# Attention sums by accumulating DMAs and column tiles of ones, in place of a third pass over the values

## The chip, the core and the metric

The kernel runs on one core of a Trainium2 chip. The metric is the device time of one execution in microseconds (us). Engines are named as the profile names them: PE (TensorE, matmuls), PEld (its weight loads), DVE (VectorE), ACT (ScalarE), POOL (GpSimd), SP (SyncE, which issues most DMAs).

## What is computed

One layer of a hybrid backbone over 128 prompt tokens and 1024 latent tokens, all in F32, width 1024. One projection gives queries, keys, values and gates of two mixers with 8 query heads of 64 and 2 key heads each (so a key head g serves 4 query heads). Mixer A is global attention, mixer B a band of 128 with a sink. The part that the change touches is mixer A:

```
def global_attn_latent(q, k_lat, v_lat, k_ctx, v_ctx):
    k_all = concatenate([k_ctx, k_lat]); v_all = concatenate([v_ctx, v_lat])    # 128 + 1024 keys
    s = einsum('bqkgd,bskd->bkgqs', qblk, k_all) * d ** -0.5                     # per block of 128 queries
    p = softmax(s, axis=-1)
    return einsum('bkgqs,bskd->bqkgd', p, v_all)
...
merge_out: concatenate([o_a * silu(g_a), o_b * silu(g_b)]) @ w_out
```

Prompt tokens attend to themselves alone, with the same weights.

## The kernel before

Matmuls take operands of type F32R. To keep F32's precision each operand is split in a high part and a low part (what is left of the value), and a product is made of several passes: high x high, high x low, low x high.

The kernel has a stage of modulation and projections (until about 303 us in the profile), the attention stage, and a short tail. Attention runs over 36 units (t, m, g): tile t of 128 tokens, mixer m (0 is A, 1 is B), key head g. For each latent tile and head an A unit is followed by a B unit; the two prompt pairs come last. A unit has 4 heads x 128 queries = 512 columns. An A unit of a latent tile has nine blocks of 128 keys, one *slot* each; a B unit has three or four. So an A unit with the B unit behind it makes a cycle of 13 slots, 12 at the first and the last latent tile.

In a slot of an A unit `scores` has TensorE make the transposed scores (keys on partitions, 512 columns) in two passes; ScalarE takes the exponential into a tile `pe` and casts it to the high part `ph`; the low part `pl` = pe - ph is made on GpSimd (L1131), for block 4 on VectorE (L1129). Three slots later (LAG) `values` runs the passes that multiply by the values and sum over all blocks in one PSUM bank `pv`. The stationary tile of A is `v_hi`: 64 columns of the values' high part, and 64 columns of ones beside them. The passes are

```
nc.tensor.matmul(pv, two, ph, start=(b == 0), stop=False)              # L1141: [values high | ones] by ph
if m == 0:
    nc.tensor.matmul(pv[0:64, :], vl, ph, start=False, stop=False)     # L1143: values low by ph, A alone
nc.tensor.matmul(pv, two, pl, start=False, stop=last)                  # L1144: [values high | ones] by pl
```

The ones give the row sums of the softmax in partitions 64 to 127 of `pv`, each of them 64 times. At a unit's end (END_AT, slots after the last block) ScalarE makes the inverse of the sums with a logarithm and an exponential (L1155, L1156), VectorE multiplies the values by it (L1165), GpSimd multiplies by the loaded gate `sgl` (L1167), ScalarE casts to `ogh` and GpSimd makes the low part `ogl` (L1179), and the output projection's passes (L1212) are laid into later slots, 2.5 a slot. For mixer B, `v_hi` has the values' high and low part side by side, two passes are enough, and the two halves of `pv` are added at the end; B's exponentials are made beside A's first four slots (`weight_items`) and its sums are handled apart. Passes that find a bound for the scores (`pmx`, L881) are laid into fixed slots.

Work is written down slot by slot: `tick()` first runs what `later(n, f)` put down for this slot, then come `scores`, what is due, output passes, and `values`. Every engine runs its instructions in the order of writing (`in_order`); an instruction that waits holds up all behind it on its engine. Buffers: PES = 3 tiles `pe`, 4 of `ph` and `pl` each, NOG = 5 pairs of gated outputs; PSUM banks A (2, small items), B (2, scores), C (2, `pv`), D and E.

Of the kernel before, what the change touches and what calls it, by code (L numbers as in the profile page):

```python
# [18 lines left out]
P = 128  # L19
# [16 lines left out]
PL_DVE = (4,)  # L36
LAG = 3
# [26 lines left out]
NOG = 5  # L64
PES = 3
# [43 lines left out]
def hybrid_step(ctx, tc, x_prompt, x_sample, cache_k_a, cache_v_a, cache_k_b, cache_v_b,  # L109
# [598 lines left out]
    v_lo = kv.tile([P, 20, HD], F32R, name="v_lo")  # L708
# [7 lines left out]
    def split_values(src, j):  # L716

        nc.vector.tensor_tensor(v_lo[:, j : j + 2, :], src[:, 0], v_hi[:, 0, j : j + 2, 0, :], op=ALU.subtract)
        nc.vector.tensor_tensor(v_hi[:, 1, j : j + 2, 1, :], src[:, 1], v_hi[:, 1, j : j + 2, 0, :], op=ALU.subtract)

    with tc.tile_pool(name="kt", bufs=2) as kt:
        W_GB.pools[WRAW : WRAW + 2] = [(kt, 2)] * 2
        sg_tile.append(lambda n: kt.tile([P, 512], F32, tag="kh", name=n, bufs=KEYS))
        for b in range(0, 20, 4):
            later(4 + b // 2, lambda b=b: nc.gpsimd.tensor_scalar(
                v_hi[:, 0, b : b + 4, 1, :], gain4, 0.0, 1.0, op0=ALU.mult, op1=ALU.add))
# [353 lines left out]
    w2 = ctx.enter_context(tc.tile_pool(name="w2", bufs=2, side="right"))  # L1080
    def blocks(t, m, g):

        if t == 0:
            k = (khp[:, g, :], klp[0:68, g, :]) if m == 0 else 0
            return [(k, v_hi[:, m, 18 + g], v_lo[:, 18 + g, :])]
        if m == 0:
            return [((kha[:, g, b, :], kla[:, g, b, :]), v_hi[:, 0, 2 * b + g], v_lo[:, 2 * b + g, :]) for b in range(9)]
        p0, p1_ = window(t)
        at = {p: b + 1 for b, p in enumerate(POS)}
        return [(p - p0, v_hi[:, 1, 2 * at.get(p, 0) + g], None) for p in range(p0, p1_)]  # L1090
# [16 lines left out]
    def scores(i, b, blk):  # L1107

        t, m, g = units[i]
        s = bank("B", f"st{i}_{b}")  # L1110
        ph, pl = parts_tiles(i, b)
        if m == 1:
            o = P * blk[0]
            for h in range(4):
                nc.tensor.transpose(s[:, P * h : P * h + P], penat[i][:, h, o : o + P], ident_r.bitcast(F32))  # L1115
            nc.scalar.copy(ph, s)  # L1116
            later(1, lambda: nc.vector.tensor_tensor(pl, s, ph, op=ALU.subtract))  # L1117
            return ph, pl
        kh, kl = blk[0]
        nc.tensor.matmul(s, kh, qtile[i], start=True, stop=False)  # L1120
        nc.tensor.matmul(s, kl, qbtile[i], start=False, stop=True)  # L1121
        pe = w3.tile([P, 512], F32, tag="pe", name=f"pe{i}_{b}", bufs=PES)
        nc.scalar.activation(pe, s, AF.Exp)  # L1123
        if i == 0 and b < PH_DVE:
            nc.vector.tensor_copy(ph, pe)
        else:
            nc.scalar.copy(ph, pe)  # L1127
        if b in PL_DVE:
            later(1, lambda: nc.vector.tensor_tensor(pl, pe, ph, op=ALU.subtract))  # L1129
        else:  # L1130
            nc.gpsimd.tensor_tensor(pl, pe, ph, op=ALU.subtract)  # L1131
        return ph, pl

    def values(i, b, last, blk, ph, pl):
        t, m, g = units[i]
        _, vh, vl = blk
# [5 lines left out]
        if m == 0:  # L1142
            nc.tensor.matmul(pv[0:64, :], vl, ph, start=False, stop=False)  # L1143
# [6 lines left out]
        def inverse():  # L1150
            v["rs"] = w2.tile([64, 512], F32, tag="rs", name=f"rs{i}", bufs=1)
            if m == 1:
                nc.scalar.copy(v["rs"], pv[64:128, :])
                return
            nc.scalar.activation(v["rs"], pv[64:128, :], AF.Ln)  # L1155
            nc.scalar.activation(v["rs"], v["rs"], AF.Exp, scale=-1.0)  # L1156

        def gated():
# [5 lines left out]
            for s in range(2):  # L1164
                nc.vector.tensor_tensor(of[64 * s : 64 * s + 64], pvv[:, :, s, :], srv[:, :, s, :],  # L1165
                                        op=ALU.add if m else ALU.mult)
            nc.gpsimd.tensor_tensor(of, of, sgl.pop(i), op=ALU.mult)  # L1167
            later(GATE_LATE, lambda: load_gate(i + 2))
            v["of"] = of
# [176 lines left out]
```

## Time and profile before

| | us |
|---|---|
| median of 2 runs (711.51 to 711.84) | 711.67 |
| the profiled execution | 711.52 |
| its span, first to last instruction | 709.6 |
| attention stage, first scores to the last latent tiles | 303 to 694 |

| engine | busy us of the span |
|---|---|
| PE | 691.6 |
| PEld | 558.5 |
| DVE | 469.3 |
| ACT | 409.9 |
| POOL | 334.2 |

Busy times are unions of the instructions' spans. TensorE's matmuls overlap, so that the duration of one (395 ns for 512 columns) is more than what it adds to a row of them; the distance between two starts tells that. DMAs count for no engine; their issue stands in the rows of the issuing queue (SPq, ACTq), with the time to landing. The granted clock of TensorE was 0.999 over the span. A row of a timeline is: start, duration, engine, line, operation, out<-in, count, and in brackets the idle time just before with the instruction that ended it.

### The profile page before, as it was taken

The numbers are of one execution on the slowest core, as the hardware profiler recorded it, in microseconds if no ns is written. First come the engines' busy times: TensorE is split into PE (matmuls) and PEld (weight loads), VectorE is DVE, ScalarE is ACT, GpSimd is POOL, SyncE is SP. The second block draws the span as 40 slices with busy tenths as digits, with TensorE's granted clock in tenths as the row PEclk, the third lists the DMA queues.
The fourth block names the chain that finished last, engine by engine and source line by source line (L and its number), as shares of the span: only waits on it lengthen the run. The fifth ranks groups of instructions, "written<-read, shape, count | busy, mean of one in ns | idle before, by whom it ended". The sixth has DMA issues, their size and how long they took to land. (4 is left out here: it accounts for less than half of the span.)

```text
span 709.6 us, 10604 instructions
## 1 busy us (share of the span) xinstructions
PE 691.6 (97%) x3508; PEld 558.5 (79%) x3508; DVE 469.3 (66%) x1019; ACT 409.9 (58%) x829; POOL 334.2 (47%) x356
## 2 busy tenths in 40 slices
PE   7999999999999999989999999999999999999987
PEld 4778988878787889966788888888888888787865
DVE  4667257967848945647867578666775776675662
ACT  5646412412403431188777887787778777877760
POOL 3547023233213421256756655665576557555660
PEclk9999999999999999999999999999999999999999
DMA  8962283358353116332222121212221221222323
GB/s 316 415 211 102 78 302 74 90 154 263 84 139 104 37 39 215 123 108 57 78 68 85 50 82 53 71 57 75 68 82 38 79 71 50 78 72 70 104 67 121
DMA packets 53560, 78.58 MB, mean 111 GB/s; under 512 B 7096, under 2 KB 25720, under 8 KB 52608
## 3 DMA queue, kind: packets, MB, share of 16 engines
q1 hardware_dynamic: 45328, 65.96, 28.1%
q10 hardware_dynamic: 8176, 11.94, 6.3%
q8 instruction: 28, 0.46, 0.3%
q14 instruction: 28, 0.23, 0.1%
HBM read 58.69 MB, written 19.18 MB: 110 GB/s over the span
## 5 line engine op out<-in xcount | busy, mean ns | idle before, releaser
L1131 POOL TENSOR_TENSOR pl<-pe,ph 128x512 fp32r<-128x512 f32 x130 | 167.7, 1292 | 145.0 <-DVE nm L942 67.5
L882 DVE TENSOR_REDUCE mx<-pmx 128x1 f32<-128x384 f32 x192 | 101.4, 552 | 56.3 <-PE pmx L881 54.8
L1123 ACT ACTIVATE pe<-st 128x512 f32<-128x512 f32 x146 | 86.8, 594 | 28.2 <-PE st L1121 27.4
L1127 ACT CAST ph<-pe 128x512 fp32r<-128x512 f32 x146 | 90.6, 621 | 4.8
L1141 PE MATMUL pv<-ph,v_hi 128*128 128x512 f32 x208 | 82.8, 398 | 2.2 <-DVE spare L1165 2.2
L1144 PE MATMUL pv<-pl,v_hi 128*128 128x512 f32 x208 | 82.4, 396 | 0.0
L1212 PE MATMUL po<-wo,ogh 128*128 128x512 f32 x216 | 72.6, 395 | 0.2 <-DVE yt L1219 0.2
L174 POOL TENSOR_TENSOR rs_q<-ms_q,mhalf 128x8 f32<-128x8 f32 x18 | 34.1, 1896 | 80.9 <-DVE ms_q L172 80.9
L942 DVE CUSTOM_DVE_ANT_0 sn<-sn,mask,nsink 128x512 f32<-128x512 f32 (+1 forms) x64 | 46.4, 724 | 38.0 <-PE sn L939 37.6
L881 PE MATMUL pmx<-kha,qt 128*128 128x384 f32 x192 | 61.2, 363 | 0.4 <-ACT pen L928 0.2
L1120 PE MATMUL st<-qt,kha 128*128 128x512 f32 x144 | 58.2, 404 | 1.9 <-ACT pe L1123 1.1
L1121 PE MATMUL st<-qb,kla 68*128 68x512 f32 x144 | 57.5, 399 | 1.1 <-DVE qb L901 1.1
L1143 PE MATMUL pv<-ph,v_lo 128*64 128x512 f32 x146 | 57.6, 395 | 0.0
L1144 PEld LDWEIGHTS pv<-pl,v_hi 128*128 128x128 f32 x208 | 39.2, 189 | 16.4
L928 ACT ACTIVATE pen<-sn,nm 128x512 f32<-128x512 f32 (+2 forms) x72 | 45.0, 626 | 6.5 <-DVE nm L942 3.1
L1116 ACT CAST ph<-st 128x512 fp32r<-128x512 f32 x62 | 36.4, 587 | 19.9 <-PE st L1115 18.7
L1141 PEld LDWEIGHTS pv<-ph,v_hi 128*128 128x128 f32 x208 | 39.3, 189 | 10.6 <-ACT ogh L1177 2.4
L646 ACT CAST qo0q<-ptq 128x512 fp32r<-128x512 f32 x18 | 10.6, 586 | 60.7 <-PE ptq L643 55.8
L1212 PEld LDWEIGHTS po<-wo,ogh 128*128 128x128 f32 x216 | 40.0, 188 | 6.8 <-DVE yt L1219 0.6
L1117 DVE TENSOR_TENSOR pl<-st,ph 128x512 fp32r<-128x512 f32 x62 | 42.5, 686 | 2.7 <-ACT ph L1116 2.1
L1212 PE MATMUL po<-wo,ogl 128*128 128x512 f32 x108 | 42.6, 394 | 0.0
L881 PEld LDWEIGHTS pmx<-kha,qt 128*128 128x128 f32 x192 | 35.6, 191 | 6.4 <-DVE mx L882 1.3
(213 smaller groups left out, 1699.2 us busy)
## 6 DMA issues: line engine op xcount, KB each, us to landing
qt<-qd SPq DMA_DIRECT2D x36, 256.0 KB, 3.0
wm<-in_w_mod_ss_dram SPq DMA_DIRECT2D x7, 1024.0 KB, 10.0
qd<-qo0q ACTq DMA_DIRECT2D x36, 128.0 KB, 2.4
qd<-qo1q ACTq DMA_DIRECT2D x36, 128.0 KB, 2.4
sgl<-gd SPq DMA_DIRECT2D x36, 128.0 KB, 2.2
out_dram<-yt SPq DMA_DIRECT2D x17, 256.0 KB, 2.0
xn<-in_x_sample_dram SPq DMA_DIRECT2D x8, 512.0 KB, 7.2
wg<-in_w_mod_g_dram SPq DMA_DIRECT2D x4, 1024.0 KB, 8.3
```

Source lines behind the costliest of these rows:

```text
L881: nc.tensor.matmul(pm[:, 0:384], lhs, kha[:, g, 3 * b : 3 * b + 3, :], start=True, stop=True)
L882: nc.vector.tensor_reduce(mx[:, h, b : b + 1], pm[:, 0:384], axis=AX.X, op=ALU.max)
L942: nc.vector.tensor_tensor_reduce(s, s, mask[:, m0 : m0 + n], -1.0, nsink[:, 4 * g + h : 4 * g + h + 1], op0=ALU.add, op1=ALU.min, accum_ou ...
L1120: nc.tensor.matmul(s, kh, qtile[i], start=True, stop=False)
L1121: nc.tensor.matmul(s, kl, qbtile[i], start=False, stop=True)
L1123: nc.scalar.activation(pe, s, AF.Exp)
L1127: nc.scalar.copy(ph, pe)
L1131: nc.gpsimd.tensor_tensor(pl, pe, ph, op=ALU.subtract)
L1141: nc.tensor.matmul(pv, two, ph, start=(b == 0), stop=False)
L1143: nc.tensor.matmul(pv[0:64, :], vl, ph, start=False, stop=False)
L1144: nc.tensor.matmul(pv, two, pl, start=False, stop=last)
L1212: nc.tensor.matmul(po[n], a, wo_parts[KT * n + k][lo], start=(k == KS[0] and p == 0), stop=(k == KS[-1] and p == 2))
```

## The change

In `v_hi` mixer A's values now stand as B's did: high part and low part side by side, with no ones. An A unit makes two passes a block, and the two halves of `pv` are added at the end for both mixers (ScalarE copies one, VectorE adds the other).

The row sums are made in another way. Two F32 tiles `acc` of 128x512 take turns. The exponentials of blocks 0 and 1 are written right into them; the tiles `pe` of blocks 2 to 8 are added to them by accumulating DMAs, SBUF to SBUF, issued from GpSimd a slot later. So `acc` holds, for each of 128 key positions, the sum over blocks. Then `row_sums` sums over partitions: the stationary tile is 128x32 of ones in F32, and four matmuls with 32 columns each fill the four quarters of a PSUM tile 128x256 (for a quarter, two of the four heads); one group for each of the two accumulators, 4 and 5 slots later (SUMS_AT). ScalarE makes the inverse with a logarithm and an exponential on 128x256, and GpSimd multiplies the gate `sgl` by it (a new product) before it multiplies the output by `sgl`. For the prompt units the one tile `pe` is summed without a DMA.

PES goes from 3 to 4, NOG from 5 to 4. The fill of ones in `v_hi` (five GpSimd instructions) becomes one memset, and the two subtractions that split the values become one.

```diff
+ADD_AFTER = 1
+PROMPT_SUMS = 2
+SUMS_AT = (4, 5)
-NOG = 5
-PES = 3
+NOG = 4
+PES = 4
...
-    v_lo = kv.tile([P, 20, HD], F32R, name="v_lo")
+    ones_v = kv.tile([P, 32], F32, name="ones_v")
...
-        nc.vector.tensor_tensor(v_lo[:, j : j + 2, :], src[:, 0], v_hi[:, 0, j : j + 2, 0, :], op=ALU.subtract)
-        nc.vector.tensor_tensor(v_hi[:, 1, j : j + 2, 1, :], src[:, 1], v_hi[:, 1, j : j + 2, 0, :], op=ALU.subtract)
+        nc.vector.tensor_tensor(v_hi[:, :, j : j + 2, 1, :], src, v_hi[:, :, j : j + 2, 0, :], op=ALU.subtract)
...
+    acc = [w2.tile([P, 512], F32, name=f"acc{n}", bufs=1) for n in range(2)]
...
-        pe = w3.tile([P, 512], F32, tag="pe", name=f"pe{i}_{b}", bufs=PES)
+        mine = acc[(i // 2 + b) % 2]
+        if t and b < 2:
+            pe = mine
+        else:
+            pe = w3.tile([P, 512], F32, tag="pe", name=f"pe{i}_{b}", bufs=PES)
         nc.scalar.activation(pe, s, AF.Exp)
...
+        if t == 0:
+            later(PROMPT_SUMS, lambda: row_sums(i, pe))
+        else:
+            later(ADD_AFTER, lambda: add_up(i, b, pe, mine))
         return ph, pl
+
+    summed, scaling = {}, {}
+
+    def add_up(i, b, pe, mine):
+        if b > 1:
+            nc.gpsimd.dma_start(mine, pe, accum_op=ALU.add)
+        if b > 6:
+            later(SUMS_AT[b - 7] - ADD_AFTER + (b == 7), lambda: row_sums(i, mine, b - 7, b == 8))
+
+    def row_sums(i, src, n=0, last=True):
+        if n == 0:
+            summed[i] = bank("A", f"ss{i}")[:, 0 : 2 * P]
+        ss = summed[i]
+        by = src.rearrange("p (c s n) -> p s c n", s=2, n=P)
+        for a in range(0, P, 32):
+            nc.tensor.matmul(ss[a : a + 32].rearrange("p (c n) -> p c n", c=2), ones_v, by[:, a // HD],
+                             start=(n == 0), stop=last, tile_position=(0, a))
+        if not last:
+            return
+        iv = w2.tile([P, 2 * P], F32, tag="iv", name=f"iv{i}", bufs=1)
+        nc.scalar.activation(iv, ss, AF.Ln)
+        nc.scalar.activation(iv, iv, AF.Exp, scale=-1.0)
+        scaling[i] = iv.rearrange("p (c n) -> p c n", c=2)
...
         nc.tensor.matmul(pv, two, ph, start=(b == 0), stop=False)
-        if m == 0:
-            nc.tensor.matmul(pv[0:64, :], vl, ph, start=False, stop=False)
         nc.tensor.matmul(pv, two, pl, start=False, stop=last)
...
-            if m == 1:
-                nc.scalar.copy(v["rs"], pv[64:128, :])
-                return
-            nc.scalar.activation(v["rs"], pv[64:128, :], AF.Ln)
-            nc.scalar.activation(v["rs"], v["rs"], AF.Exp, scale=-1.0)
+            nc.scalar.copy(v["rs"], pv[64:128, :])
...
+            v["of"] = of
+            if t and m == 0:
+                later(1, gate_on)
+            else:
+                gate_on()
+
+        def gate_on():
+            if m == 0:
+                nc.gpsimd.tensor_tensor(sgl[i], sgl[i], scaling.pop(i), op=ALU.mult)
+            nc.gpsimd.tensor_tensor(v["of"], v["of"], sgl.pop(i), op=ALU.mult)
             later(GATE_LATE, lambda: load_gate(i + 2))
```

How the instructions now stand on two engines is shown at two places. The first is GpSimd in the second half of an A unit of a middle tile, from the subtraction of block 5 to the end. `pl_5` is the low part of block 5, `ogl` the low part of a gated output, `spare` the gated outputs themselves; before the change:

```order
L1131 TENSOR_TENSOR pl_5_4845<-pe_5_4848,ph_5_4844 128x512 [waits PE_49,Activation_49]
L1167 TENSOR_TENSOR spare<-spare,sgl_4613 128x256 [waits DVE_49]
L974 TENSOR_TENSOR sum_4738<-sum_4738,ex_4739 128x4 [waits Activation_49]
L1131 TENSOR_TENSOR pl_6_4871<-pe_6_4874,ph_6_4870 128x512 [waits PE_49,Activation_49]
L1131 TENSOR_TENSOR pl_7_4885<-pe_7_4888,ph_7_4884 128x512 [waits PE_49,Activation_49]
L1131 TENSOR_TENSOR pl_8_4913<-pe_8_4916,ph_8_4912 128x512 [waits PE_49,Activation_49]
L1179 TENSOR_TENSOR ogl_4907<-spare,ogh_4906 128x256 [waits Pool_49]
```

And the same place after it, where `DMASW` stands for the landing of a DMA issued from GpSimd:

```order
L1136 TENSOR_TENSOR pl_5_5472<-pe_5_5475,ph_5_5471 128x512 [waits PE_49,Activation_49]
L1202 TENSOR_TENSOR spare<-spare,sgl_5231 128x256 [waits DVE_49]
L974 TENSOR_TENSOR sum_5364<-sum_5364,ex_5365 128x4 [waits Activation_49]
L1147 DMA acc_3357<-pe_5_5475 128x512 [waits DMASW2_49]
L1136 TENSOR_TENSOR pl_6_5498<-pe_6_5501,ph_6_5497 128x512 [waits PE_49,Activation_49]
L1147 DMA acc_3358<-pe_6_5501 128x512 [waits DMASW3_49]
L1136 TENSOR_TENSOR pl_7_5512<-pe_7_5515,ph_7_5511 128x512 [waits PE_49,Activation_49]
L1147 DMA acc_3357<-pe_7_5515 128x512 [waits DMASW4_49]
L1136 TENSOR_TENSOR pl_8_5540<-pe_8_5543,ph_8_5539 128x512 [waits PE_49,Activation_49]
L1213 TENSOR_TENSOR ogl_5533<-spare,ogh_5532 128x256 [waits Pool_49]
L1147 DMA acc_3358<-pe_8_5543 128x512 [waits DMASW7_49,DMASW5_49]
```

Four DMA issues have come between the subtractions, and each waits for the landing of the one before it on its accumulator, two blocks back. The second place is TensorE around the start of the next A unit, whose first scores are `st_0`; before the change:

```order
L881 MATMUL pmx_1_1_6760<-kha,qt_6586 128x384 [waits DVE_49]
L1212 MATMUL po_0_6739<-wo_0_3036,ogl_6569 128x512
L1212 MATMUL po_0_6739<-wo_1_3061,ogh_6568 128x512
L1212 MATMUL po_0_6739<-wo_1_3062,ogh_6568 128x512
L1141 MATMUL pv_6766<-ph_0_6686,v_hi 128x512
L1144 MATMUL pv_6766<-pl_0_6687,v_hi 128x512
L1120 MATMUL st_0_6772<-qt_6293,kha 128x512 [waits DVE_49,PE_49]
L1121 MATMUL st_0_6772<-qb_6713,kla 128x512 [waits DMAHW7_49]
```

And after it, where `ss` are the row sums of the A unit just ended:

```order
L881 MATMUL pmx_1_1_4436<-kha,qt_4259 128x384 [waits DVE_49]
L1246 MATMUL po_0_4412<-wo_0_3022,ogl_4243 128x512
L1246 MATMUL po_0_4412<-wo_1_3047,ogh_4242 128x512
L1246 MATMUL po_0_4412<-wo_1_3048,ogh_4242 128x512
L1173 MATMUL pv_4442<-ph_0_4361,v_hi 128x512
L1174 MATMUL pv_4442<-pl_0_4362,v_hi 128x512
L1157 MATMUL ss_4417<-acc_3358,ones_v 32x256 [waits DMASW3_49]
L1157 MATMUL ss_4417<-acc_3358,ones_v 32x256 x3
L1121 MATMUL st_0_4455<-qt_3951,kha 128x512 [waits DVE_49]
L1122 MATMUL st_0_4455<-qb_4387,kla 128x512 [waits DMAHW7_49]
```

The second group of sums stands ahead of the next unit's first scores and waits for the landing of the last accumulating DMA; the first group stands one slot earlier.

More of the change, by code (lines that the diff above doesn't have):

```diff
@@ L723, in hybrid_step @@
         sg_tile.append(lambda n: kt.tile([P, 512], F32, tag="kh", name=n, bufs=KEYS))
-        for b in range(0, 20, 4):
-            later(4 + b // 2, lambda b=b: nc.gpsimd.tensor_scalar(
-                v_hi[:, 0, b : b + 4, 1, :], gain4, 0.0, 1.0, op0=ALU.mult, op1=ALU.add))
+        later(4, lambda: nc.gpsimd.memset(ones_v, 1.0))
         ones = ident_r.bitcast(F32)[64:68].unsqueeze(1)
```

12 lines of the change are left out of this document (5 added, 7 removed).

## The prediction

> **What bounds the kernel now.** I read the page's busy times first, then a table of engine times by stretch, then the timelines of TensorE, ScalarE and GpSimd through one cycle of the attention stage.
>
> ```profile
> span 709.6 us, 10604 instructions
> PE 691.6 (97%) x3508; PEld 558.5 (79%) x3508; DVE 469.3 (66%) x1019; ACT 409.9 (58%) x829; POOL 334.2 (47%) x356
> 303.20:694.00 390.80, 384.21 (x1843) 305.36 (x1842) 261.70 (x563) 307.31 (x624) 237.78 (x257) 1.00 0.23 71
> 487.12:510.99 23.87, 23.87 (x116) 19.21 (x115) 15.27 (x34) 18.73 (x37) 14.09 (x15) 1.00 0.21 67
> ```
>
> The two last rows give a stretch, its length, and the busy time of PE, PEld, DVE, ACT and POOL. Everything that the change moves in number lies in the attention stage, 303 to 694. The last row is one cycle there: from the first exponential of a mixer A unit to that of the next, nine slots of A and four of B. TensorE has no idle time in it; ScalarE is busy 18.73 of 23.87 us, GpSimd 14.09. So TensorE sets the pace. Its rows are pipelined, so a pass costs the distance of two starts and not its own length:
>
> ```profile
> 501.55 0.39 PE L1141 MATMUL pv<-ph,v_hi 128*128 128x512 f32 x1
> 501.77 0.39 PE L1143 MATMUL pv<-ph,v_lo 128*64 128x512 f32 x1
> 502.00 0.40 PE L1144 MATMUL pv<-pl,v_hi 128*128 128x512 f32 x1
> 502.24 0.41 PE L1120 MATMUL st<-qt,kha 128*128 128x512 f32 x1
> ```
>
> From 501.55 to 502.24 there are three passes: 0.23 us each.
>
> **What the change takes from TensorE, and gives it.** The middle pass goes:
>
> ```profile
> L1143 PE MATMUL pv<-ph,v_lo 128*64 128x512 f32 x146 | 57.6, 395 | 0.0
> 13.29 1.07 PE L346 MATMUL pm<-wm,sil 128*32 128x256 f32 x16
> 14.29 0.66 PE L390 MATMUL px<-ident,xn 128*128 128x128 f32 x4
> 151.54 0.39 PE L251 MATMUL pq<-whiqb,h 128*128 128x512 f32 x1
> 151.86 1.92 PE L596 MATMUL pgate<-wg,sil32g 128*32 128x512 f32 x16
> 153.72 0.66 PE L643 MATMUL ptq<-ident_r,qfq 128*128 128x128 f32 x4
> ```
>
> 146 passes at 0.23 us are 33.6 us, 9 x 0.23 = 2.07 in a cycle. In their place stand 34 groups of four F32 column tiles of 256 columns (two in each of 16 units, one in each of two prompt units). The kernel has such tiles elsewhere. Four groups of 256 columns take 14.29 - 13.29 = 1.00 us with what follows, four of 512 columns 153.72 - 151.86 = 1.86. With a fixed part F and g for 256 columns, F + 4g = 1.00 and F + 8g = 1.86, so g = 0.215 and F = 0.14; the way in costs 151.86 - 151.54 - 0.23 = 0.09 more. A lone group thus costs 0.445 us, two in a cycle 0.89. If nothing else ended last, the cycle would take 23.87 - 2.07 + 0.89 = 22.69 us.
>
> **What it gives GpSimd.** In a cycle GpSimd gets one more product of 128x256 and issues seven accumulating DMAs (blocks 2 to 8); each stands right behind the subtraction of its block and is issued in GpSimd's order. TensorE's second group of sums waits for the landing of block 8's DMA, and the scores of the next unit stand behind it. So a chain now runs through a unit, and I follow it in this cycle, in us from its first exponential at 487.12:
>
> ```profile
> 487.12 0.60 ACT L1123 ACTIVATE pe<-st 128x512 f32<-128x512 f32 x1 [0.48 <-PE st L1121]
> 488.45 1.29 POOL L1131 TENSOR_TENSOR pl<-pe,ph 128x512 fp32r<-128x512 f32 x1 [6.09 <-DVE nm L942]
> 490.43 1.29 POOL L1131 TENSOR_TENSOR pl<-pe,ph 128x512 fp32r<-128x512 f32 x1 [0.70 <-ACT ph L1127]
> 491.71 0.62 ACT L1127 CAST ph<-pe 128x512 fp32r<-128x512 f32 x1
> 491.68 0.73 POOL L986 TENSOR_TENSOR sgl<-sgl,spare 128x256 f32<-128x256 f32 x1
> 495.34 1.30 POOL L1131 TENSOR_TENSOR pl<-pe,ph 128x512 fp32r<-128x512 f32 x1 [0.97 <-POOL pl L1131]
> 504.24 1.29 POOL L1131 TENSOR_TENSOR pl<-pe,ph 128x512 fp32r<-128x512 f32 x1 [0.69 <-ACT ph L1127]
> 508.20 0.40 PE L1144 MATMUL pv<-pl,v_hi 128*128 128x512 f32 x1
> 510.99 0.60 ACT L1123 ACTIVATE pe<-st 128x512 f32<-128x512 f32 x1 [0.49 <-PE st L1121]
> L1131 POOL TENSOR_TENSOR pl<-pe,ph 128x512 fp32r<-128x512 f32 x130 | 167.7, 1292 | 145.0 <-DVE nm L942 67.5 <-ACT ph L1127 57.4 <-POOL pl L1131 11.2
> L1167 POOL TENSOR_TENSOR spare<-spare,sgl 128x256 f32<-128x256 f32 x36 | 26.5, 737 | 3.3 <-DVE spare L1165 2.3 <-POOL ogl L1179 0.6
> L960 POOL TENSOR_TENSOR ex<-nm,sink 128x4 f32<-128x4 f32 x18 | 3.6, 200 | 1.6 <-DVE nm L955 1.6
> ```
>
> Now, block 8's subtraction (504.24) is over 2.7 us before TensorE reads it (508.20). After the change, with X for one DMA issue on GpSimd and L from an issue's start to its landing:
> - Block 2's subtraction can start at 492.38, behind L986 and the cast that ends at 492.33; it takes 1.29, and the two gate products that now follow it 0.74 each: 495.15, which is 8.03 into the cycle. ScalarE sets this part at about 2 us a slot, and it stays.
> - From there GpSimd has no gap: blocks 3, 5, 6, 7 and 8 at 1.29 are 6.45, one more gate product and two subtractions of 128x256 are 2.22, two small steps 0.40, and seven issues 7X. It ends at 17.10 + 7X, and the last DMA lands at 17.10 + 6X + L.
> - Behind that stand a group of sums, 0.445, and ScalarE's logarithm and exponential of 128x256 ahead of the next unit's first exponential. I take 0.40 for each, from the cast of this size below, so 0.80.
>
> The cycle by this chain is 18.35 + 6X + L. It is longer than TensorE's 22.69 from 6X + L = 4.34 on, and than the 23.87 of now from 5.52 on. No DMA is issued from GpSimd in this trace, so both unknowns are bounded by the nearest rows:
>
> ```profile
> L861 SPq DMA_DIRECT2D qt<-qd x36: 332/432/592, 267.6 to 669.5; - x36
> DMA to landing us min/median/max: 2.6/3.0/4.9
> qb<-qd SPq DMA_DIRECT2D x18, 128.0 KB, 2.7
> out_dram<-yt SPq DMA_DIRECT2D x17, 256.0 KB, 2.0
> L1177 ACT CAST ogh<-spare 128x256 fp32r<-128x256 f32 x36 | 14.4, 402 | 1.5 <-POOL spare L1167 1.5
> ```
>
> For X: SyncE issues a transfer of the same 128 rows of 2 KB in 0.33 at the least and 0.43 in the median; GpSimd needs 1.29 to go over such a tile once. GpSimd has to do for each row what SyncE's queue has done for it, so I take the middle, 0.86. For L: from 2.0 (such a tile stored) to 4.9 (the longest load of one). The median load is 3.0; 128 KB more cost 3.0 - 2.7 = 0.3, and the adding transfer reads the 256 KB of its target too, so I take 3.0 + 0.6 = 3.6. Both values are estimates. The Trainium skill, DMA: Bandwidth & Descriptors, section Latency and other measured facts, gives about 1 us to the first byte on the gpsimd path against about 0.6 from SP or ACT, and puts it down to the work of GpSimd's cores; no run here shows it yet, and with X = 1.0 the sum would be 0.84 us a cycle higher, 777 us.
>
> **The sum.** 18.35 + 5.16 + 3.6 = 27.11 us, 3.24 over 23.87. The cycles of the four units of the first and last latent tiles have one B slot less and are not alike; I charge them the same. 16 x 3.24 = 51.8 us. The span would be 709.6 + 51.8 = 761.4; the profiled execution took 711.52, which is 1.9 over its span and within 0.2 of the median of 711.67. That makes 763 us.
>
> **Edits at nothing.** The buffers of the exponentials (3 to 4) must now wait for landings too: block 8 takes the buffer of block 4, whose DMA would start at 11.98 (8.03 + 2X + 1.29 + 0.20 + 0.74) and land at 15.6, while block 8's exponential stands at 502.91 - 487.12 = 15.8. Each of these DMAs also waits for the one before it on its accumulator, with the next subtraction queued behind and TensorE's last pass of that block behind that; block 2's lands at 8.03 + 3.6 = 11.6, just ahead of block 4's. At L = 4.9 it would land at 12.9, block 4's at 17.8, and ScalarE would wait 2 us, still ahead of GpSimd's turn for block 8 at 20.2. One buffer pair less for gated outputs (5 to 4) only lets output products go earlier. ScalarE swaps two passes of 64x512 for a copy of 64x512 and two of 128x256, about even. The fill of ones and the split of values lie in the projection stage under matmuls.
>
> ```profile
> 502.91 0.60 ACT L1123 ACTIVATE pe<-st 128x512 f32<-128x512 f32 x1 [0.43 <-PE st L1121]
> ```
>
> **Rivals.** *TensorE stays the bound (faster).* If an issue costs GpSimd no more than SyncE's cheapest, 0.33, and a landing about 2.3, then 6X + L = 4.3 and the chain hides; the cycle is 22.69, the gain 16 x 1.18 = 18.9, less 0.4 for the prompt units (two groups of 0.445 in, two passes of 0.23 out): 18.5 us, 693. For it: GpSimd has 9.8 us idle in the cycle. Against it: of that idle time 6.09 + 0.70 + 0.97 = 7.8 us lie behind block 8 or ahead of block 3, where they shorten no chain. The Trainium skill, DMA: Bandwidth & Descriptors, section Anatomy of one DMA — SWDGE (gpsimd) path, speaks for this rival: it calls descriptor generation small and variable and puts a transfer at about 2.0 us plus bytes over 436 GB/s, by which 256 KB would land in an estimated 2.6; only the changed kernel can show it. *Even.* With SyncE's median values, 0.43 and 3.0, 6X + L is 5.6 and the cycle 23.9: 713 us. *The tiles do not run side by side.* If the four column tiles of a group, which here read two runs of 128 columns each, went one after another, a group would cost 4 x 0.215 + 0.23 = 1.09, two of them 2.18 against the 2.07 saved: 711 + 2 = 713 us even with a cheap issue. The rows of L346 and L596 speak against it.
>
> **Chances.** My forecast, the chain through GpSimd, 0.63. TensorE stays the bound: 0.20, of which 0.03 fall short of 2%. Even: 0.12. Tiles one by one: 0.05. Two per cent is about what a measurement of this kernel can tell from no change; so faster 0.17, same 0.03 + 0.12 + 0.05 = 0.20, slower 0.63. The forecast's own range goes from X = 0.6, L = 3.0 (24.95 us a cycle, 729 us) to X = 1.1, L = 4.2 (29.15, 796). The extremes of the rows, 1.29 and 4.9, would give 31.0 and 825. The range over all cases is 694 to 800; half of the fastest case and the dearest issues are left out.
>
> **What would show it.** The page of the changed kernel should list 112 issues of accumulating DMAs on GpSimd, and a GpSimd timeline without gaps from block 3 on, with X as the distance between a subtraction's end and the next start. TensorE should stand idle ahead of the sums, released by a DMA, for 3 us or more in a cycle, and the distance of first exponentials should be about 27 us. I am wrong if that distance is 23 or less with TensorE busy throughout, if the sums wait for nothing, or if the gap is in ScalarE's wait for buffers.

## The result, and the profile after

The changed kernel takes 846.6 us (843.6 to 849.7) against 711.7: a ratio of 1.189, interval 1.185 to 1.192. Slower was the likeliest case of the prediction, but its 763 us are far too low and the time lies outside its range of 694 to 800.

The changed kernel in the same views: the span, the busy times, then the groups of instructions, the queue and the issues that answer to the rows shown of before.

```profile
span 847.9 us, 11115 instructions
PE 740.1 (87%) x3634; PEld 561.5 (66%) x3634; DVE 490.8 (58%) x1009; ACT 410.3 (48%) x847; POOL 445.3 (53%) x482
L1136 POOL TENSOR_TENSOR pl<-pe,ph 128x512 fp32r<-128x512 f32 x98 | 162.9, 1668 | 5.4 <-ACT ph L1132 5.3
L1147 POOL DMA_DIRECT2D acc<-pe x112 | 123.1, 1103 | 21.5 <-DMA acc<-pe 6.2 <-PE st L1116 4.4 <-PE pmx L881 3.8
L1174 PE MATMUL pv<-pl,v_hi 128*128 128x512 f32 x208 | 91.4, 439 | 45.9 <-POOL pl L1136 38.8 <-DVE m_nat L895 6.7
L1157 PE MATMUL ss<-acc,ones_v 128*32 128x256 f32 x256 | 27.3, 506 | 35.7 <-DMA acc<-pe 35.2 <-DVE wo_big L1038 0.6
q0 software_dynamic: 16128, 29.37, 19.3%
acc<-pe POOLq DMA_DIRECT2D x112, 256.0 KB, 4.1
```

TensorE's share of the span has fallen from 97% to 87%. The sums (L1157) have waited 35.2 us for landings, 2.2 us a cycle where the prediction looked for 3 or more, and TensorE's last pass of a block (L1174) has waited another 38.8 us for GpSimd's subtractions. The subtractions on GpSimd (L1136) show 1.67 us in place of 1.29, since their spans overlap those of the issues. The last row gives the median landing of an accumulating DMA: 4.1 us, where the prediction took 3.6. That median mixes two groups: in the ten cycles below, the DMAs of blocks 2 to 4 land 3.9, 3.8 and 3.3 us after their issue in the mean, those of blocks 5 to 8, of which the last two release the sums, 5.5, 5.2, 4.9 and 4.8.

The same ten A units of the middle of the stage, from the first exponential of one to that of the eleventh, in the table of engine times by stretch (length, then busy PE, PEld, DVE, ACT, POOL, then the granted clock), before and after:

```profile
367.82:606.46 238.64, 238.64 (x1151) 192.16 (x1150) 164.72 (x351) 187.31 (x370) 140.90 (x150) 1.00 0.22 67
```

```profile
393.26:714.19 320.93, 265.13 (x1222) 192.05 (x1221) 175.52 (x350) 187.62 (x382) 209.46 (x230) 0.91 0.50 107
```

A cycle has gone from 23.86 to 32.09 us. TensorE had no idle time in these ten cycles and now has 55.8 us; its clock is 0.91 of full speed. One such cycle, 549.87 to 583.81, in the timelines of ScalarE, GpSimd and TensorE of the changed kernel:

```profile
549.87 0.58 ACT L1128 ACTIVATE acc<-st 128x512 f32<-128x512 f32 x1
564.70 1.20 POOL L1147 DMA_DIRECT2D acc<-pe  x1
565.32 1.88 POOL L1136 TENSOR_TENSOR pl<-pe,ph 128x512 fp32r<-128x512 f32 x1
566.54 1.52 POOL L1147 DMA_DIRECT2D acc<-pe  x1
567.16 2.21 POOL L1136 TENSOR_TENSOR pl<-pe,ph 128x512 fp32r<-128x512 f32 x1
570.51 0.90 POOL L1147 DMA_DIRECT2D acc<-pe  x1 [1.13 <-PE st L1116]
573.02 1.20 POOL L1147 DMA_DIRECT2D acc<-pe  x1
572.76 0.50 PE L1174 MATMUL pv<-pl,v_hi 128*128 128x512 f32 x1 [1.35 <-POOL pl L1136]
577.43 1.08 PE L1157 MATMUL ss<-acc,ones_v 128*32 128x256 f32 x8 [4.17 <-DMA acc<-pe]
578.44 0.27 PE L900 MATMUL ptm<-ident_r,m_nat 128*4 128x128 f32 x1
582.23 0.77 PE L1157 MATMUL ss<-acc,ones_v 128*32 128x256 f32 x8
583.81 0.58 ACT L1128 ACTIVATE acc<-st 128x512 f32<-128x512 f32 x1
```

The issues at 564.70, 566.54, 570.51 and 573.02 are those of blocks 5 to 8. Block 7's, which the program lets wait for the landing of block 5's on the same accumulator and for nothing else, goes out 5.8 us after that one, behind 1.13 us of idle GpSimd (the row names a TensorE instruction). The first group of sums needs block 7's landing and starts 6.9 us after that issue, with TensorE idle for 4.17 us. A whole slot of passes stands between it and the second group, which begins 4.80 us later and shows no idle time ahead of it; block 8's landing, which the prediction took for the deciding one, is not what it waits for: in the mean of the ten cycles it lands 2.1 us ahead of that group.

The mean over ten such cycles, worked out from the starts in these timelines (us from the unit's first exponential), beside the prediction's terms:

| | last DMA issued | first sums | second sums | next first exponential |
|---|---|---|---|---|
| prediction | 22.26 (17.10 + 6X) | - | 25.86 (+ L) | 27.11 |
| changed kernel | 23.54 | 26.00 | 30.45 | 32.09 |

### The profile page after: what moved, and what is told of

Its sections match the earlier page's. It is cut to its first block, busy times and chain, and to the rows that moved or that the text cites. A ratio compares the mean times of both kernels' runs of the same rounds, so it can differ in the third digit from the quotient of the medians.

```text
span 847.9 us, 11115 instructions
## 1 busy us (share of the span) xinstructions
PE 740.1 (87%) x3634; PEld 561.5 (66%) x3634; DVE 490.8 (58%) x1009; ACT 410.3 (48%) x847; POOL 445.3 (53%) x482
## 4 chain that ended last, share of the span: by engine, by line
PE 56%; POOL 17%; DMA 14%; issue 7%; DVE 4%; ACT 1%; ACTq 0%; SPq 0%; POOLq 0%; DVEq 0%
DMA acc<-pe 12%; PE po L1246 8%; POOL pl L1136 6%; POOL acc L1147 6%; PE pq L254 4%; PE pq L252 4%; PE pq L253 4%; PE ss L1157 3%; PE pg L266 3%; PE pg L262 3%; PE pg L267 3%; PE pv L1173 2%; PE pv L1174 2%; PE st L1121 2%; PE st L1122 2%
## 5 line engine op out<-in xcount | busy, mean ns | idle before, releaser
L1136 POOL TENSOR_TENSOR pl<-pe,ph 128x512 fp32r<-128x512 f32 x98 | 162.9, 1668 | 5.4 <-ACT ph L1132 5.3
L1147 POOL DMA_DIRECT2D acc<-pe x112 | 123.1, 1103 | 21.5 <-DMA acc<-pe 6.2
L1174 PE MATMUL pv<-pl,v_hi 128*128 128x512 f32 x208 | 91.4, 439 | 45.9 <-POOL pl L1136 38.8
L882 DVE TENSOR_REDUCE mx<-pmx 128x1 f32<-128x384 f32 x192 | 101.4, 552 | 42.1 <-PE pmx L881 39.2
L1136 POOL TENSOR_TENSOR pl<-acc,ph 128x512 fp32r<-128x512 f32 x32 | 41.1, 1286 | 141.6 <-PE pv L1174 88.1
L1174 PEld LDWEIGHTS pv<-pl,v_hi 128*128 128x128 f32 x208 | 41.7, 200 | 72.8 <-POOL pl L1136 65.6
L1246 PE MATMUL po<-wo,ogh 128*128 128x512 f32 x216 | 79.1, 427 | 0.1
L1128 ACT ACTIVATE pe<-st 128x512 f32<-128x512 f32 x114 | 67.7, 594 | 20.1 <-DMA acc<-pe 17.9
L1132 ACT CAST ph<-pe 128x512 fp32r<-128x512 f32 x114 | 70.7, 620 | 3.9
L1157 PE MATMUL ss<-acc,ones_v 128*32 128x256 f32 x256 | 27.3, 506 | 35.7 <-DMA acc<-pe 35.2
L901 DVE TENSOR_TENSOR qb<-ptm,diag 4x512 fp32r<-4x512 f32 x18 | 12.3, 682 | 74.3 <-PE ptm L900 74.3
L1246 PEld LDWEIGHTS po<-wo,ogh 128*128 128x128 f32 x216 | 44.7, 210 | 7.9 <-DVE yt L1253 0.6
```

Of the source, the lines that this page charges most:

```text
L882: nc.vector.tensor_reduce(mx[:, h, b : b + 1], pm[:, 0:384], axis=AX.X, op=ALU.max)
L1147: nc.gpsimd.dma_start(mine, pe, accum_op=ALU.add)
L1157: nc.tensor.matmul(ss[a : a + 32].rearrange("p (c n) -> p c n", c=2), ones_v, by[:, a // HD], start=(n == 0), stop=last, tile_position=(0, a))
L1246: nc.tensor.matmul(po[n], a, wo_parts[KT * n + k][lo], start=(k == KS[0] and p == 0), stop=(k == KS[-1] and p == 2))
```

## The experiments

All ratios are to the kernel before on the same chip (711.6 to 712.5 us). The quoted lines of the runs are of the same views as above.

**What each part costs: four steps from before to after.** The first run keeps only the missing third pass:

```diff
-            nc.gpsimd.dma_start(mine, pe, accum_op=ALU.add)
+            pass
...
-            nc.tensor.matmul(ss[a : a + 32].rearrange("p (c n) -> p c n", c=2), ones_v, by[:, a // HD],
...
+        ss = src[:, 0 : 2 * P]
...
-        nc.scalar.activation(iv, ss, AF.Ln)
+        nc.scalar.copy(iv, ss)
```

> Left out: the accumulating DMAs and all the column-tile matmuls; the scaling is made from one block's exponentials by a copy in place of Ln, so that the operations of ScalarE and GpSimd stay. What is left of the change is the third value pass that is gone. Theory A, the removed passes are worth what the prediction summed (33.6 us) and the sums themselves cost the rest: 712 - 33.6 plus up to 8 us that a later end showed in the run without DMAs, so 680 to 690 us, against 726 with the sums in: the sums would then cost 36 to 46 us, more than the passes gave. Theory B, a chain of other engines sets the 23.87 us cycle before, so that a pass is worth less than its 0.23 us: 705 us or more.

Measured: 698.7 us, 0.980 (0.976 to 0.984), between the two. The second run puts the sums back and leaves out the DMAs alone:

```diff
-            nc.gpsimd.dma_start(mine, pe, accum_op=ALU.add)
+            pass
```

> The changed kernel without its 112 accumulating DMAs; the sums then run over blocks 0, 1 only (the additions of blocks 2 to 8 are left out, the groups of sums stay). Theory landing (TensorE waits at the first group of sums for the landing of block 7's DMA, and its clock drops after the wait): 693 us, 23 us a cycle, no wait ahead of the sums, clock full. Rival GpSimd time (the issues fill GpSimd and make the subtractions late): the same 693, since the issues are gone too. Rival tiles (the column tiles or the new product cost the time): still 800 or more.

Measured: 726.4 us, 1.020 (1.018 to 1.022), 33 us over the 693 of the first two theories and far under the third. Even with additions that cost nothing this change would have been slower than the kernel before. Ten cycles of each, the first run and then the second:

```profile
371.42:593.48 222.06, 221.56 (x1061) 179.01 (x1060) 162.41 (x351) 188.40 (x381) 147.23 (x160) 1.00 0.23 72
```

```profile
397.17:638.83 241.66, 237.98 (x1222) 181.90 (x1221) 162.35 (x350) 187.38 (x382) 147.40 (x160) 1.00 0.21 65
```

The sums add 1.96 us to a cycle that had 22.21. TensorE's timeline in the second run shows why two groups are not 0.89 us:

```profile
512.82 0.39 PE L1174 MATMUL pv<-pl,v_hi 128*128 128x512 f32 x1
513.13 0.64 PE L1157 MATMUL ss<-acc,ones_v 128*32 128x256 f32 x8
513.70 0.22 PE L900 MATMUL ptm<-ident_r,m_nat 128*4 128x128 f32 x1
513.76 0.62 PE L1116 MATMUL st<-ident_r,pen 128*128 128x128 f32 x4
514.70 0.44 PE L881 MATMUL pmx<-kha,qt 128*128 128x384 f32 x1 [0.31 <-DVE qb L901]
```

A group of four tiles is eight rows, so each of these F32 products counts twice; from 512.82 + 0.23 to 513.70 it takes 0.65 us. Behind it TensorE stands still ahead of `pmx` for 0.31 us: `ss` now holds one of the two banks A that `pmx` and `ptm` take in turn. (That the bank is the cause is argued; it was not tried with another bank.)

The third run has the DMAs, but TensorE's sums read a tile of ones, so that only GpSimd and the buffers meet the landings; the row sums are thus not those of the exponentials. Blocks 0 and 1 use ordinary buffers, and the accumulators are cleared once.

```diff
-        if t and b < 2:
+        if False:
...
-            nc.tensor.matmul(ss[a : a + 32].rearrange("p (c n) -> p c n", c=2), ones_v, by[:, a // HD],
+            nc.tensor.matmul(ss[a : a + 32].rearrange("p (c n) -> p c n", c=2), ones_v, ones_v[:, 0:2].unsqueeze(2).to_broadcast([P, 2, P]),
```

> The changed kernel with its DMAs, but nobody on TensorE waits for them: the sums run over the constant tile of ones, and blocks 0 and 1 use ordinary buffers (so the scaling is left out in effect). GpSimd still issues 112 DMAs and waits for the one two blocks back. Theory landing: most of the loss goes, 700 to 730 us, about 23 to 24.5 us a cycle, clock near full. Rival GpSimd time: the loss stays, 800 to 850 us, and TensorE's last pass of a block still waits for the subtraction.

Measured: 794.0 us, 1.115 (1.112 to 1.118), between the two theories and nearer to GpSimd time. Its waits (total, times, longest):

```profile
PEld pv L1176 <- POOL pl L1138: 65.0, 53, 2.5
PE pv L1176 <- POOL pl L1138: 37.0, 33, 2.1
ACT pe L1130 <- DMA acc<-pe: 16.1, 17, 2.0
```

TensorE now waits for GpSimd's subtractions; the kernel before has no such row among its waits. So the ladder is: third pass out, -13.4 us; sums in, +27.7; DMAs in, +67.6; their landings waited for on TensorE, +52.6; together 135.

**What the DMAs hold up.** The kernel before, with all three passes, and the same seven DMAs a unit beside it, into tiles that nobody reads (the third pass reads one small tile in place of the values' low parts, at the same width):

```diff
-NOG = 5
-PES = 3
+NOG = 4
+PES = 4
...
+        if t and b > 1:
+            mine = acc[(i // 2 + b) % 2]
+            later(1, lambda: nc.gpsimd.dma_start(mine, pe, accum_op=ALU.add))
```

> The kernel before with three value passes, and 7 accumulating DMAs a unit of 9 blocks into two tiles that nobody reads; 4 buffers for exponentials and 4 for outputs, as in the kernel after; the third pass reads a small tile in place of the low parts of the values, at the same width. Theory A, the DMAs hold GpSimd up inside the nine slots in which it also has a subtraction each: with two passes they cost 68 us (794 against 726); a slot with a third pass is 0.23 us longer, 2.1 us in a unit and 33 us in 16 units, so some 745 us. Theory B, they cost only where somebody waits for a landing: nobody reads these sums, so under 722 us.

Measured: 750.5 us, 1.053 (1.050 to 1.057): theory A, 38 us with nobody waiting for a sum. Beside two passes the same DMAs cost 68: the third pass gives each slot, in which GpSimd has a subtraction and an issue to fit in, 0.23 us more. The traces bear this out. The last issue stands at nearly the same place of the mean cycle, 23.04 us here and 23.33 beside two passes. Without DMAs TensorE came to its last pass of block 8 at 21.08 us with three passes (508.20 in the cycle of the prediction) and at 18.95 with two (512.82, above, in a cycle that began at 493.87), so beside two passes the same chain of GpSimd holds it up by some 2 us a cycle more.

Plain copies in place of adding ones (no sums are formed, and the logarithm becomes a copy):

```diff
-            nc.gpsimd.dma_start(mine, pe, accum_op=ALU.add)
+            nc.gpsimd.dma_start(mine, pe)
...
-        nc.scalar.activation(iv, ss, AF.Ln)
+        nc.scalar.copy(iv, ss)
```

> The changed kernel with plain copies from GpSimd in place of adding ones (the additions are left out, and the logarithm is a copy of the same size so that no infinity arises); every wait stays. If the long landing comes from the adding (two reads, 176 ns a packet): landing falls from 4.1 us to about 3, 760 to 790 us. If it comes from GpSimd's issue and its queue: landing stays at 4 or more, 830 to 850 us. Rival GpSimd time: no change, 840 to 850.

Measured: 778.1 us, 1.093 (1.085 to 1.100), in the range of the first case. Its rows:

```profile
L1136 POOL TENSOR_TENSOR pl<-pe,ph 128x512 fp32r<-128x512 f32 x98 | 127.0, 1296 | 7.5 <-ACT ph L1132 5.9
L1147 POOL DMA_DIRECT2D acc<-pe x112 | 64.3, 574 | 6.7 <-DMA acc<-pe 3.7 <-PE pv L1174 1.5 <-PE st L1122 1.0
q0 software_dynamic: 8960, 29.37, 9.7%
acc<-pe POOLq DMA_DIRECT2D x112, 256.0 KB, 3.1
```

The same bytes land in 3.1 us in place of 4.1, in 80 packets a DMA in place of 144, and take half the time of the queue: 0.097 x 780.9 / 112 = 0.68 us of all 16 engines for each, against 0.193 x 847.9 / 112 = 1.46. The adding itself thus costs 69 of the 135 us. Only a quarter of the columns added:

```diff
-            nc.gpsimd.dma_start(mine, pe, accum_op=ALU.add)
+            nc.gpsimd.dma_start(mine[:, 0:P], pe[:, 0:P], accum_op=ALU.add)
```

> The kernel after, but each accumulating DMA adds only 128 of the 512 columns (64 KB in place of 256 KB, still one row for each of the 128 partitions), so three quarters of the sums are not complete. Theory A, GpSimd's part (issue and the subtractions behind it) goes by the count of rows and stays: the landing gets some 1.5 us shorter, the waits of TensorE at the sums shrink, and the time comes to that of the run in which nobody waits for a landing: 790 to 805 us. Theory B, the bytes also set how long GpSimd is held: 770 us or less.

Measured: 804.3 us, 1.130 (1.123 to 1.136), theory A's number, but not by its way alone: the landing is 3.1 us too, and GpSimd's last issue comes at 21.40 in the mean cycle in place of 23.54 (plain copies: 21.06). The 2.1 us are waits of DMAs for the DMA two blocks before them. In the mean of the ten cycles block 4's issue comes 2.63 us after block 3's in the changed kernel and 2.04 here, block 7's 3.94 after block 6's and 2.58 here, and the other steps from issue to issue agree within 0.04. GpSimd's idle time ahead of all issues is 21.5 us there and 2.0 here (the rows put 6.2 and 0.4 of it down to a landing by name):

```profile
L1147 POOL DMA_DIRECT2D acc<-pe x112 | 145.5, 1308 | 2.0 <-PE pmx L881 1.2 <-DMA acc<-pe 0.4 <-issue 0.3
```

So without these waits an issue costs (21.40 - 17.10) / 6 = 0.72 us on GpSimd, with plain copies 0.66, if the 17.10 of the prediction is right. All additions on VectorE:

```diff
-            nc.gpsimd.dma_start(mine, pe, accum_op=ALU.add)
+            nc.vector.tensor_tensor(mine, mine, pe, op=ALU.add)
```

> The changed kernel with the additions on VectorE (112 of 128x512 with two SBUF inputs) in place of the DMAs; all computed. Theory landing and rival GpSimd time: TensorE bound again, 693 to 705 us, VectorE busy 15.3 + 7 x 0.69 = 20.1 of 22.7 us a cycle. If VectorE's adds and GpSimd's subtractions hold each other up: 710 to 740 us, GpSimd's subtraction above 1.29 us.

Measured: 783.8 us, 1.101 (1.099 to 1.103): a miss of 80 us. The additions take 1.01 us in the mean in place of the 0.69 that was expected. The group row and the waits:

```profile
L1147 DVE TENSOR_TENSOR acc<-acc,pe 128x512 f32<-128x512 f32 x112 | 111.9, 1011 | 3.7 <-ACT pe L1128 2.4 <-issue 0.8
```

```profile
PEld pmx L881 <- DVE mx L882: 43.0, 53, 2.6
PE pmx L881 <- DVE mx L882: 26.8, 33, 2.2
```

The maxima that bound mixer A's scores (L882) stand behind the additions on VectorE, and TensorE's next products for them (`pmx`) wait. Before, it was VectorE that waited for these products (54.8 us in all, against 0.2 the other way). How much of the loss is the slower addition and how much the order was not tried.

**Where the wait ends last.** Two runs move some additions to VectorE, the early or the late ones:

```diff
-            nc.gpsimd.dma_start(mine, pe, accum_op=ALU.add)
+            if b < 6:
+                nc.vector.tensor_tensor(mine, mine, pe, op=ALU.add)
+            else:
+                nc.gpsimd.dma_start(mine, pe, accum_op=ALU.add)
```

> The kernel after, but blocks 2 to 5 are added by VectorE and only blocks 6, 7 and 8 by DMAs: four issues a unit fewer on GpSimd, in slots in which VectorE has no maxima to take; the last landing stays where it was. Theory A, GpSimd's part in the block slots and the landing at the end each hold a share: 7 DMAs that nobody waited for cost 68 us (794 against 726), four of them are 39 us, so 800 to 815 us. Theory B, the landing ahead of the sums decides alone: 835 us or more. Theory C, it is GpSimd alone, and relieved of four issues it is also in time at the end: under 785 us.

Measured: 817.1 us, 1.146 (1.143 to 1.149), a little above theory A's range. The other run has `b > 6` in place of `b < 6`:

> The kernel after, but the last two additions of a unit (blocks 7 and 8) are done by VectorE, and blocks 2 to 6 by DMAs: no group of sums comes right behind a landing. Theory A: the landing's share goes (847 - 794 = 53 us) and two issues a unit on GpSimd (2/7 of 68 us, 19 us); two additions among VectorE's maxima come in their place (2/7 of the 58 us that seven of them cost over the run without additions, 17 us): 785 to 800 us. Theory B, the wait at the landing only covers a lateness that comes from GpSimd in the slots before: 815 us or more. Theory C, additions among the maxima cost more than their share: 815 us or more too, with waits of the passes behind VectorE's maxima to tell it from B.

Measured: 860.9 us, 1.208 (1.205 to 1.210), slower than the change itself. The landing did not go away:

```profile
DVE acc L1148 <- DMA acc<-pe: 94.0, 16, 6.7
PE pmx L881 <- DVE mx L882: 81.4, 13, 7.0
```

VectorE's first late addition waits 5.9 us in the mean for the DMA before it on its accumulator, and the maxima queue up behind it. It is theory C's place, the maxima, but a wait that none of the three had named: the landing moved to an engine with more behind it. Fewer subtractions on GpSimd:

```diff
-PL_DVE = (4,)
+PL_DVE = (2, 4, 6)
```

> The kernel after, with all its DMAs; VectorE makes the low parts of blocks 2, 4 and 6 in place of those of block 4 alone: two subtractions a unit fewer on GpSimd. Theory A, GpSimd's chain sets the time, as the prediction had it: two subtractions of 1.3 to 1.7 us, 2.6 to 3.3 us in a cycle, 42 to 53 us in all, so 795 to 805 us. Theory B, landing and clock set it: 835 us or more.

Measured: 821.1 us, 1.152 (1.149 to 1.155), half of what theory A expected: the last issue comes 0.8 us earlier (22.72), the cycle is 1.45 us shorter. Both groups of sums at the later slot (in three of the 16 units, those with 12 slots ahead of another A unit, the late group's start falls 0.65 to 1.54 us after the next unit's first exponential, and it reads a tile into which these have been written; the expectations speak of one):

```diff
-SUMS_AT = (4, 5)
+SUMS_AT = (5, 5)
```

> The kernel after, with the first group of sums put off by one slot, so that both stand side by side at the later place and the DMA of block 7 has a slot longer to land. Theory A, the first group's wait is one of its own (4.17 us in the cycle that was read, with a second one behind it): it goes, and 1 to 2 us of 32 in each cycle, 820 to 832 us. Theory B, the prediction's place: block 8's landing decides, and the first group only waits where the second would: 842 to 852 us.

Measured: 827.5 us, 1.161 (1.154 to 1.167), theory A. With both groups there, block 8's landing decides in the mean cycle, as the prediction had it, but it takes 4.88 us and not 3.6, and the second group starts 4.98 us after that DMA's issue. Both edits at once:

> The kernel after with both edits that helped: the low parts of blocks 2, 4 and 6 on VectorE (26 us gained by itself) and both groups of sums at the later slot (19 us by itself; in one of the 16 units the late group then reads a tile into which the next unit's first exponentials have been written). Theory A, they are two costs in a row, GpSimd's chain up to the last issue and what stands behind it: both go, 847 - 45, 795 to 808 us. Theory B, both only give block 7's DMA more time to land, so that the second finds nothing left: 815 to 825 us.

Measured: 800.3 us, 1.123 (1.119 to 1.126): 46 us, about the sum of the two (25.5 + 19.1). GpSimd's chain up to the last issue and the first group's wait behind it are separate costs, one after the other.

**What half clock costs.** The granted clock shows 103.6 us at half speed in the changed kernel, in 18 stretches, nearly all of 3.41 or 6.83 us, against 2.9 us before. Passes that do nothing were put ahead of the first group:

```diff
...
+        rest = summed[i][:, 2 * P : 4 * P]
+        for _ in range(20 if n == 0 and units[i][0] else 0):
+            nc.tensor.matmul(rest, ident_r, v_hi[:, 0, 0:2].rearrange("p j s d -> p (j s d)"), start=True, stop=True)
...
```

> The kernel after with 20 more passes of 256 columns (about 0.12 us each, 2.4 us) on TensorE ahead of the first group of sums of each unit, into the unused half of their bank: TensorE is busy through half of its wait. Theory A, the half clock that follows each wait of about 4 us costs time: half clock falls from 104 us to under 30 us, and the time to 815 to 830 us. Theory B, the half clock falls into time in which TensorE waits for GpSimd anyway: 842 to 852 us, whatever the clock does.

Measured: 841.4 us, 1.180 (1.175 to 1.186), by the time theory B. But half clock was still 56.0 us, the slot between the groups had gone from 4.45 to 3.32 us, and the first sums came at 26.76 in place of 26.00: the passes did not fit into the wait. With 10 of them:

> The kernel after with 10 passes of 256 columns ahead of the first sums in place of the 20 of the run before, so that they fit into the wait. Of the mean cycle of 32.1 us the slot between the two groups of sums took 4.45 us, with nobody to wait for the landing 3.31 us; with 20 passes it took 3.32 us, and the first sums came 0.7 us later. Theory A, half clock costs the 1.1 us: with 10 passes the first sums stand where they stood and the slot is the short one, 1.1 us by 16 cycles less: 826 to 834 us. Theory B, half clock is a companion of the wait and not a cost: 842 to 850 us.

Measured: 831.4 us, 1.169 (1.165 to 1.173), theory A. First sums at 25.80, the slot 3.52 us, half clock 32.4 us, and ten cycles in

```profile
390.88:698.52 307.64, 265.60 (x1322) 199.53 (x1321) 174.96 (x350) 187.81 (x381) 209.42 (x230) 0.97 0.52 112
```

13.3 us less than without. Half clock costs some 15 us, and work without any use gives them back. The Trainium skill, TensorE: Matmul & The Clock Gate, section HAM oscillation — how this bites in real kernels, has the rule: a wait above about 3.4 us drops the clock, and the work behind it starts slow each time. The trace agrees with the second half, and with the stretches of 3.41 us, but not with the length of the wait: of the waits in the attention stage only three are above 3.4 us (4.17, 3.49 and 4.29, all ahead of first groups), and there are 18 stretches. Here is one behind two short waits in the changed kernel:

```profile
606.84 0.50 PE L1174 MATMUL pv<-pl,v_hi 128*128 128x512 f32 x1 [1.14 <-POOL pl L1136]
609.02 0.64 PE L1157 MATMUL ss<-acc,ones_v 128*32 128x256 f32 x8 [1.68 <-DMA acc<-pe]
609.80:613.20 3.40, 3.37 (x11) 2.18 (x9) 2.53 (x4) 0.59 (x1) 0.00 (x0) 0.51 0.32 58
```

Short waits alone, then, do not keep a kernel from half clock.

**Buffers.** The kernel before with the buffer counts of the change (`NOG = 4`, `PES = 4`):

> The kernel before with 4 output buffers in place of 5 and 4 buffers for exponentials in place of 3, as the change has them, and nothing else. Theory A, the buffers cost nothing, as the prediction had it: 709 to 715 us. Theory B, they cost at the front and the end of the attention stage: 717 us or more.

Measured: 711.7 us, 1.000 (0.999 to 1.002), theory A. And the passes alone with the counts of before (`NOG = 5`, `PES = 3`):

> The run with the passes alone (no DMAs, no column-tile sums, 698.7 us), with the buffers of before: 5 for outputs, 3 for exponentials. That run began its third unit 4.8 us later than the kernel before and had 61.6 us left from its last unit's first exponentials, against 57.6. Theory A, the buffers hold these 8 us: 688 to 693 us. Theory B, TensorE does not set the pace at the front and at the end, so that a pass removed there gains nothing: 696 to 701 us.

Measured: 700.5 us, 0.985 (0.983 to 0.986), theory B's number: the buffers are not why the passes give so little. At the front of the attention stage TensorE was not the bound even in the kernel before, as its row there shows (17.93 us busy of 20):

```profile
306.00:326.00 20.00, 17.93 (x82) 12.72 (x83) 9.39 (x22) 17.98 (x39) 13.30 (x13) 1.00 0.32 94
```

The mean cycle of the main runs, put together from the same starts as above, over ten cycles (over eleven of 13 slots in the rows "nobody waits" and "narrow additions"):

| run | last DMA issued | to first sums | to second sums | to next exponential | cycle |
|---|---|---|---|---|---|
| changed kernel | 23.54 | 2.46 | 4.45 | 1.64 | 32.09 |
| nobody waits for a landing | 23.33 | 0.16 | 3.31 | 1.46 | 28.27 |
| plain copies | 21.06 | 1.54 | 3.67 | 1.48 | 27.75 |
| narrow additions | 21.40 | 2.60 | 3.74 | 1.45 | 29.19 |
| 10 passes ahead of the sums | 23.44 | 2.36 | 3.52 | 1.45 | 30.76 |
| fewer subtractions on GpSimd | 22.72 | 2.63 | 3.82 | 1.48 | 30.64 |
| sums side by side, later | 23.89 | 3.11 | 1.87 | 1.75 | 30.62 |

## Why the prediction was wrong, step by step

- **The direction and the first part of the mechanism** held. A chain through GpSimd's subtractions and issues sets the cycle; there are 112 issues; TensorE stands idle ahead of the sums, released by a DMA. The sign is partly luck: it would have come out even without the chain, since with the DMAs left out the change is a loss too (726.4).
- **The chain up to the last issue, 17.10 + 6X**, was 1.28 us too short, with two errors that partly cancel: 22.26 forecast, 23.54 measured. X = 0.86 was too high (0.72), 0.84 us too much over six issues. The waits of DMAs for the one before them on their accumulator, which the text worked out and put at nothing because block 2's would land in time, cost 2.1 us (23.54 - 21.40): that step used L = 3.6 for DMAs that stand apart and looked at block 2's alone, and block 5's needed 5.5 in the mean.
- **L, from the last issue to the sums, is the term that failed**, together with what stands behind it. The prediction let one landing (3.6) and 1.25 us of sums, logarithm and exponential follow the last issue: 4.85. It took 8.55. The deciding landing is not block 8's but block 7's: its sums stand a slot earlier, and the slot's own passes, which the prediction left out, stand behind them. With no landing waited for, the same stretch takes 4.93 us, of which 3.31 are that slot. The landing adds 2.30 on top, the slot grows by 1.14 (0.93 of it goes with the ten passes that keep the clock up, so it is mostly half clock), and the last part by 0.18. The text read from the order that the first group stood "one slot earlier" and drew no time from it.
- **The clock** was in no term and in no rival, though a forecast wait of 3 us or more lay beside a trace with a granted clock in it: about 15 us.
- **The sum.** The cycle was 4.98 us too short. 16 x 4.98 = 79.7 us on 761.4 make 841 of the 847.9 us of span; the other 7 lie in the first and last units, which were charged like the rest.
- **33.6 us for the third pass** were 13.4. In ten middle cycles 238.64 - 222.06 = 16.6 us of the 20.7 were gained; up to the first of these cycles the run is 3.6 us later than before, and from the end of the ten cycles to the end it takes 1.1 us more. Buffers are excluded as the reason. Where TensorE has idle time, as at the front, a pass removed is not worth its length; what holds the front up instead was not tried.
- **0.445 us for a group of sums** was 0.65. The sixteen rows read as four groups elsewhere in the kernel were two, as an F32 product stands twice in the trace; read so, the same rows give g = 0.43 and 0.14 + 0.43 + 0.09 = 0.66 for a lone group. Sums in cost 27.7 us where 15.1 (34 x 0.445) were put.
- **The rival at 693 us**, TensorE stays the bound, had no room: with the DMAs left out altogether the time is 726. It was given a chance of 0.20 on two mis-sized terms of the same kind, the third pass and the sums.
- **Tiles one after another** priced a group at 1.09 us; 0.65 speaks for tiles that overlap.
- **The Trainium skill's two figures** are of DMA: Bandwidth & Descriptors, sections Latency and other measured facts and Anatomy of one DMA — SWDGE (gpsimd) path. The first, about 1 us to the first byte, was tried as X = 1.0, against 0.72 by the narrow additions; it is a time to the first byte and not one that GpSimd is held. The landing estimated from the second was 2.6 us, against 3.1 measured for plain copies and 4.1 for adding ones.
- **The range** missed because X and L were varied, each within its rows, with the structure held fixed. Its outer point of 825 us had the same missing slot.

## What to carry to other kernels

An accumulating DMA is not a free adder: look first for what its issuing engine must do in those very slots, then for its landing in a queue of its like, not standing alone, and then for every instruction between the first wait and the end of the chain. Price the replacement by itself before the helper: here the sums cost twice what the removed pass gave back, so that with the sums in these places no way of adding could have made the change pay. When a landing must be waited for, put the reader where little is queued behind it; moved to another engine in order, the same wait cost more.

## What the runs showed of the hardware that was not expected

Beside the packets of an adding DMA, the half clock and its cure, told above:

- An issue of an accumulating DMA shows 1.10 us on GpSimd and lengthens the subtraction behind it (1.67 in place of 1.29), while their starts are only 0.62 apart (564.70 to 565.32); an issue of a plain copy shows 0.57 and leaves the subtraction at 1.30.
- The VectorE addition of two 128x512 tiles took from 0.68 to 1.82 us, 0.94 in the median of one window of 60 us, in the run with all additions there.
